# Row 5's last 640 columns are loaded by two transfers of their own

## The chip, the cores and the metric

The kernel runs on one core of one Trainium2 chip. The metric is the device time of one execution in microseconds, as the median of several runs. Before the change it is 1247.63 us, with three runs between 1247.31 and 1247.77 us.

## The reference

`logits` is 8 x 1024 x 8192 in float32 and `labels` is 8 x 1024 in int32 (they reach the kernel as 64-bit numbers). The result is the gradient of the cross entropy with respect to the logits, one softmax per row of 8192, with one subtracted at the label.

```python
logits_max = np.max(logits, axis=-1, keepdims=True)
exp_logits = np.exp(logits - logits_max)
softmax = exp_logits / np.sum(exp_logits, axis=-1, keepdims=True)
...
one_hot[batch_idx, seq_idx, labels] = 1.0

return (softmax - one_hot).astype(np.float32)
```

There are 8192 rows of 32 KB. Each is read once and written once, 268 MB each way.

## The kernel before, in words

The 8192 rows are taken 128 at a time, one row in each of the 128 partitions. What follows calls such a block of 128 x 8192 numbers (4 MB) a tile row, and counts them with t from 0 to 63. The wording of the change, "row 5", means the tile row t = 5. Two neighbouring tile rows, of parity j = 0 and 1, hold neighbouring rows of the logits.

The on-chip buffer `X` has six places (`SLOTS` = 3 times `G` = 2, so `R` = 6) of 32 KB in each partition. Tile row t uses place k = t % 6. Everything happens in place: a load fills it, VectorE finds the maximum of each row (`row_max`), ScalarE writes the exponentials over the logits and sums them (`row_exp`), VectorE inverts the sum (`invert`), ScalarE multiplies by the inverse (`row_scale`), VectorE subtracts one where the column number is the label (`subtract`), and a store sends it to the output.

All instructions are put out by one helper, `run` (in the profile nearly all of them are listed under line 67, where the helper calls the engine). It takes a list of waits; the last of them is carried by the instruction itself and each one ahead of it is an instruction of its own on the same engine. Then it lets the instruction count a semaphore up, by 16 for a transfer and by 1 for all else.

Each engine runs its own list in order:

- SP (SyncE) issues the 64 loads, in the order of t (`load`). From t = 6 on, each waits until the store from its place has landed (`put`). Tile rows 0 to 4 wait for nothing. Tile row 5 waits for VectorE, since the column numbers were first made in the first half of its place (`made`), from which VectorE copies them to PSUM (`iota`).
- VectorE makes the table of labels and the column numbers, then `row_max(0)`, and then passes a loop of ten rounds of six tile rows: `invert(k)`, `row_max` of the next tile row, `subtract(k)`. `row_max(5)` comes once in each round, at k = 4. Its load is awaited through the semaphore `got[2][1]`, against a count kept in a register.
- ScalarE runs `row_scale(k)` and `row_exp` of the next tile row, and issues the stores on its own queue.
- The last four tile rows, 60 to 63, stand behind the loop. The very last is scaled and subtracted in quarters and stored in two halves of 2 MB.

The names that the change touches are `load`, `row_max`, the line that makes the semaphores, and two constants at the head of the file (`LAST` is used nowhere).

Of the kernel before, what the change touches and what calls it, by code (L numbers as in the profile page):

```python
# [7 lines left out]
P = 128  # L8
G = 2
SLOTS = 3  # L10
R = SLOTS * G


LAST = 4


@with_exitstack
def kernel(
# [6 lines left out]
    nc = tc.nc  # L25
# [8 lines left out]
    N, V = x_nv.shape  # L34
# [3 lines left out]
    x_b = x_nv.rearrange("(b p j) v -> b p j v", p=P, j=G)  # L38
# [17 lines left out]
    with tc.tile_critical():  # L56
        sem = tc.alloc_semaphore
        got = [[sem(f"got{i}{q}") for q in range(2)] for i in range(SLOTS)]
        put = [[sem(f"put{i}{q}") for q in range(2)] for i in range(SLOTS)]
        lab_got, dve, pe, pool = (sem(n) for n in ("lab_got", "dve", "pe", "pool"))  # L60
        count = {}

        def run(engine, waits, counter, method, **operands):

            for w in waits[:-1]:
                engine.wait_ge(*w)
            instruction = getattr(engine, method)(**operands)  # L67
            for w in waits[-1:]:
                instruction._wait_ge(*w)
            step = 16 if method == "dma_start" else 1  # L70
            instruction.then_inc(counter, step)
            count[counter.name] = count.get(counter.name, 0) + step
            return counter, count[counter.name]
# [6 lines left out]
            out=ident[:], in_=ident[:], compare_op=Alu.not_equal, fill=1.0,  # L80
# [10 lines left out]
        for j in range(G):  # L91
            w = run(
                nc.tensor, [w_ident, w_lab], pe, "transpose",
                out=lab_ps[:, j, :], in_=lab_f[:, j, :], identity=ident[:],
# [4 lines left out]
            out=iota[:].bitcast(i32), in0=made.bitcast(i32), scalar1=0, scalar2=None, op0=Alu.bitwise_or,  # L99
# [6 lines left out]
        max_of, exp_of, inv_of, scl_of, sub_of = map(per_parity, ("max", "exp", "inv", "scl", "sub"))  # L106

        def slot(k):
            return X[:, k // G, k % G, :]

        def column(a, k):
            return a[:, k : k + 1]

        def load(t):
            b, j = divmod(t, G)
            k = t % R
            after = [(put[k // G][q], t // R * 16) for q in range(G)] if t >= R else []
            after = after[j : j + 1] or [w_iota] * (t == R - 1)
            run(nc.sync, after, got[k // G][j], "dma_start", out=slot(k), in_=x_b[b, :, j, :])

        def row_max(k, n):
            run(
                nc.vector, [(got[k // G][k % G], n)], max_of[k % G], "tensor_reduce",
                out=column(m, k), in_=slot(k), axis=mybir.AxisListType.X, op=Alu.max, negate=True,
            )

# [37 lines left out]
        for t in range(T):  # L164
            load(t)

        row_max(0, 16)
        row_exp(0, 1)

        done = [counter(nc.vector, q + 1) for q in range(SLOTS)]  # L170
        landed = counter(nc.vector, 16)
        with nc.vector.Fori(0, ROUNDS * SLOTS, SLOTS) as b:  # L172
            for k in range(R):
                invert(k, done[k // G])
                if k == R - 1:
                    nc.vector.reg_add(landed, landed, 16)
                row_max((k + 1) % R, landed)
                subtract(k, done[k // G], lab[:, k % G, bass.ds(b + k // G, 1)])
            for reg in done:
                nc.vector.reg_add(reg, reg, SLOTS)  # L180
# [13 lines left out]
        for t in range(ROUNDS * R, T - 1):  # L194
            k, n = t % R, t // G + 1
            invert(k, n)
            row_max(k + 1, 16 * (ROUNDS + 1))
            row_scale(k, n)
            row_exp(k + 1, n + k % G)
            subtract(k, n, lab[:, t % G, t // G : t // G + 1])  # L200
            store(k, n, o_b[t // G, :, t % G, :])
        k, n = (T - 1) % R, B
        invert(k, n)
        for q in range(4):
            c = slice(q * V // 4, (q + 1) * V // 4)
# [41 lines left out]
```

## Time and profile before

| What | Before |
|---|---|
| median of three runs | 1247.63 us |
| lowest and highest | 1247.31 and 1247.77 us |
| span of the profiled execution, first to last instruction | 1245.6 us |
| ACT: busy time | 919.4 us, 74% of the span |
| loads on SP's queue | 64 of 4096 KB |
| stores on ACT's queue | 63 of 4096 KB and 2 of 2048 KB |

The profile is of one execution, whose own time outside the profiler is not listed; its span stands 2.0 us below the median of the runs, which also count what lies around the span. The page gives busy times by engine, the span in 40 equal slices of 31.1 us, the DMA queues with their packets, and groups of instructions. A "landing" is the moment at which the last piece of a transfer has been counted on its semaphore. In the tables by stretch, a DMA packet is counted in the stretch in which it starts, so a share of the DMA engines can exceed 1.00 in a short stretch.

### The profile page before, as it was taken

To read this page: it belongs to the slowest core of one execution; us is meant where nothing else is said; L and a number is where in the kernel's file an instruction comes from. 1 tells how busy PE (TensorE), PEld (TensorE's weight loads), DVE (VectorE), ACT (ScalarE), POOL (GpSimd) and SP (SyncE) were. 2 spreads that over 40 slices of the span, in tenths; PEclk is the share of its full clock that TensorE was granted. 3 is DMA by queue.
4 is the path that set the end of the run, shared out by engine and by line. 5 is a ranking of instruction groups with operands and counts; after the bars stand their busy time and mean duration, and the time that the engine had idled before them with its cause. 6 is when DMAs were issued, how large, how long until landed. Compare 5 with 4: busy or idle time off the path is not lost.

```text
span 1245.6 us, 868 instructions
## 1 busy us (share of the span) xinstructions
PE 0.4 (0%) x2; PEld 0.3 (0%) x2; DVE 1121.8 (90%) x198; ACT 919.4 (74%) x196; POOL 7.4 (1%) x7
## 2 busy tenths in 40 slices
PE   0000000000000000000000000000000000000000
PEld 0000000000000000000000000000000000000000
DVE  5999999999988989889898898988988989889893
ACT  3888888888767777777767777677777777777772
POOL 2000000000000000000000000000000000000000
DMA  9999999999999999999999999999999999999999
GB/s 406 418 426 436 438 434 425 438 438 429 429 438 436 427 434 438 435 426 436 438 432 426 438 438 428 430 438 435 428 434 438 434 427 436 437 434 426 438 436 389
DMA packets 18625, 536.95 MB, mean 431 GB/s; under 512 B 2080, under 2 KB 2080, under 8 KB 2112
## 3 DMA queue, kind: packets, MB, share of 16 engines
q1 hardware_dynamic: 9216, 268.44, 50.0%
q10 hardware_dynamic: 9408, 268.51, 49.9%
q14 instruction: 1, 0.01, 0.0%
HBM read 268.50 MB, written 268.44 MB: 431 GB/s over the span
## 4 chain that ended last, share of the span: by engine, by line
another core or an unknown queue 67%; DVE 21%; DMA 6%; issue 2%; SPq 1%; DVEq 0%; ACT 0%; ACTq 0%; PE 0%
DVE m L67 11%; DVE X L67 10%; DMA out_dram<-X 4%; DMA X<-in_logits_dram 2%; SPq L67 1%; DVE iota L67 0%; DVE lab_f L67 0%; DMA lab_raw<-in_labels_dram 0%; DVEq L56 0%; ACT X L67 0%; DVE r L67 0%; PE iota L67 0%; ACTq L67 0%; DVEq L172 0%
## 5 line engine op out<-in xcount | busy, mean ns | idle before, releaser
L67 DVE TENSOR_REDUCE m<-X 128x1 f32<-128x8192 f32 x64 | 555.6, 8681 | 90.6 <-DMA X<-in_logits_dram 90.6
L67 ACT ACTIVATE X<-X,m 128x8192 f32<-128x8192 f32 x64 | 455.8, 7122 | 184.8 <-DVE m L67 184.8
L67 DVE SCALAR_TENSOR_TENSOR X<-iota,lab,X 128x8192 f32<-128x8192 int16 (+1 forms) x67 | 559.8, 8360 | 2.4 <-ACT X L67 2.4
L67 ACT ACTIVATE X<-X,r 128x8192 f32<-128x8192 f32 (+1 forms) x67 | 456.4, 6816 | 118.2 <-DVE r L67 118.2
L67 DVE RECIPROCAL r<-s 128x1 f32<-128x1 f32 x64 | 9.8, 153 | 7.3 <-ACT X L67 7.3
L67 ACT ACTIVATION_READ_ACCUMULATOR X<-X,m 128x1 f32 x64 | 11.9, 186 | 0.0
L67 DVE CAST lab_f<-lab_raw 32x256 f32<-32x256 int32 x1 | 3.8, 3784 | 4.6 <-DMA lab_raw<-in_labels_dram 4.6
L67 POOL IOTA X<- 128x8192 int16 x1 | 6.9, 6943 | 0.0
L67 DVE TENSOR_SCALAR iota<-X 128x4096 int32<-128x4096 int32 x1 | 4.4, 4428 | 0.1
L67 ACT ACT_TABLE_LOAD x1 | 1.3, 1283 | 1.4 <-SPq L56 1.4
L67 DVE COPY lab<-iota 128x64 f32<-128x64 f32 x1 | 0.2, 225 | 0.5 <-PE iota L67 0.5
L67 PE MATMUL iota<-ident,lab_f 32*128 32x32 f32 x2 | 0.4, 298 | 8.5 <-DVE lab_f L67 8.5
L67 PEld LDWEIGHTS iota<-ident,lab_f 32*128 32x128 f32 x2 | 0.3, 192 | 8.4 <-DVE lab_f L67 8.4
L67 POOL TENSOR_SCALAR_AFFINE_SELECT ident<-ident 32x32 f32<-32x32 f32 x1 | 0.2, 202 | 0.1
L67 POOL MEMSET ident<- 32x32 f32 x1 | 0.1, 114 | 0.5 <-SPq L56 0.5
L231 POOL MEMSET const-bfloat16-1.0<- 128x1 bf16 x1 | 0.1, 107 | 0.0
L231 POOL MEMSET const-uint8-127<- 128x1 uint8 x1 | 0.1, 107 | 0.0
L231 POOL MEMSET const-float32-0.0<- 128x1 f32 x1 | 0.1, 104 | 0.2 <-issue 0.2
L231 POOL MEMSET const-float32-1.0<- 128x1 f32 x1 | 0.1, 104 | 0.0
## 6 DMA issues: line engine op xcount, KB each, us to landing
X<-in_logits_dram SPq DMA_DIRECT2D x64, 4096.0 KB, 24.2
out_dram<-X ACTq DMA_DIRECT2D x63, 4096.0 KB, 55.2
out_dram<-X ACTq DMA_DIRECT2D x2, 2048.0 KB, 16.9
lab_raw<-in_labels_dram ACTq DMA_DIRECT2D x1, 64.0 KB, 3.7
```

What stands on the lines that cost most here:

```text
L67: instruction = getattr(engine, method)(**operands)
L231: nc = _bacc.Bacc("TRN2", target_bir_lowering=False, num_devices=1)
```

## The change: what it does

Tile row 5's first load (t = 5) brings columns 0 to 7551 of all 128 partitions. Two more transfers on SP's queue, directly behind it, bring columns 7552 to 8191: one for partitions 0 to 119 (120 pieces of 2560 bytes, 307,200 bytes) and one for partitions 120 to 127 (8 pieces of 2560 bytes, 20,480 bytes). Both count a new semaphore, `rest_got`, to 32 in all. `row_max(5)` waits for that 32 ahead of its old wait, in every round of the loop, though the semaphore is filled only once. All other loads of the kernel, those of the same place in later rounds among them, are as before.

```diff
-LAST = 4
+SLAB = 640
+MOST = 120
...
-        lab_got, dve, pe, pool = (sem(n) for n in ("lab_got", "dve", "pe", "pool"))
+        lab_got, dve, pe, pool, rest_got = (sem(n) for n in ("lab_got", "dve", "pe", "pool", "rest_got"))
...
-            run(nc.sync, after, got[k // G][j], "dma_start", out=slot(k), in_=x_b[b, :, j, :])
+            c = slice(0, V - SLAB) if t == R - 1 else slice(0, V)
+            run(nc.sync, after, got[k // G][j], "dma_start", out=slot(k)[:, c], in_=x_b[b, :, j, c])
+            if t == R - 1:
+                c = slice(V - SLAB, V)
+                for p in (slice(0, MOST), slice(MOST, P)):
+                    run(nc.sync, [], rest_got, "dma_start", out=slot(k)[p, c], in_=x_b[b, p, j, c])

         def row_max(k, n):
-            run(
-                nc.vector, [(got[k // G][k % G], n)], max_of[k % G], "tensor_reduce",
+            rest = [(rest_got, 32)] if k == R - 1 else []
+            run(
+                nc.vector, rest + [(got[k // G][k % G], n)], max_of[k % G], "tensor_reduce",
                 out=column(m, k), in_=slot(k), axis=mybir.AxisListType.X, op=Alu.max, negate=True,
             )
```

## The prediction

> **What bounds the kernel now.** The page comes first: its busy times, slices and queues.
>
> ```profile
> span 1245.6 us, 868 instructions
> PE 0.4 (0%) x2; PEld 0.3 (0%) x2; DVE 1121.8 (90%) x198; ACT 919.4 (74%) x196; POOL 7.4 (1%) x7
> ...
> GB/s 406 418 426 436 438 434 425 438 438 429 429 438 436 427 434 438 435 426 436 438 432 426 438 438 428 430 438 435 428 434 438 434 427 436 437 434 426 438 436 389
> DMA packets 18625, 536.95 MB, mean 431 GB/s; under 512 B 2080, under 2 KB 2080, under 8 KB 2112
> ...
> q1 hardware_dynamic: 9216, 268.44, 50.0%
> q10 hardware_dynamic: 9408, 268.51, 49.9%
> ...
> L67 DVE TENSOR_REDUCE m<-X 128x1 f32<-128x8192 f32 x64 | 555.6, 8681 | 90.6 <-DMA X<-in_logits_dram 90.6
> ```
>
> VectorE is busy 90%, but the 16 DMA engines carry loads (q1) and stores (q10) for 50.0% + 49.9% of their span. Every slice but the first and the last runs at 418 to 438 GB/s. By rounds of six tile rows (6 x 8.39 MB = 50.3 MB) the rate does not move at all; the third and the ninth round:
>
> ```profile
> 332.35:448.53 116.18, 0.00 (x0) 0.00 (x0) 104.50 (x19) 86.02 (x18) 0.00 (x0) 1.00 1.00 433
> ...
> 1029.40:1145.58 116.18, 0.00 (x0) 0.00 (x0) 104.39 (x19) 85.95 (x19) 0.00 (x0) 1.00 1.00 433
> ```
>
> The columns are length, busy us of PE, PEld, DVE, ACT and POOL, the granted clock, the DMA share and GB/s: 1.00 and 433 in both. That is 433 / 16 = 27.06 GB/s for one DMA engine, my price of a byte below.
>
> Next come the waits (us in total, times, longest) of SP and of VectorE, the first maximum that waited for a load, and the landings in the steady part of the run (loads first, then stores):
>
> ```profile
> SPq L67 <- DMA out_dram<-X: 1140.4, 58, 57.2
> ...
> DVE m L67 <- DMA X<-in_logits_dram: 90.6, 47, 2.0
> ...
> 307.22 8.69 DVE L67 TENSOR_REDUCE m<-X 128x1 f32<-128x8192 f32 x1 [0.54 <-DMA X<-in_logits_dram]
> ...
> DMA to landing us min/median/max: 24.2/24.2/24.3
> ...
> DMA to landing us min/median/max: 55.1/55.2/55.3
> ```
>
> SP always has a load ready and waits for a store to land. A load lands 24.2 us after its issue and a store 55.2 us, while a tile row takes 116.18 / 12 = 9.7 us of the DMA engines one way. So more than one load and several stores stand in the queues at any time. Compute could be tens of microseconds later without emptying them. The end is therefore set by bytes: the sixteen engines run without pause from the first load on, and the slowest of them ends the kernel.
>
> How far the slowest lies behind is seen in the last stores, in stretches of 0.05 us:
>
> ```profile
> 1242.85:1242.90 0.05, 0.00 (x0) 0.00 (x0) 0.00 (x0) 0.00 (x0) 0.00 (x0) 1.00 0.76 328
> 1242.90:1242.95 0.05, 0.00 (x0) 0.00 (x0) 0.00 (x0) 0.00 (x0) 0.00 (x0) 1.00 1.53 655
> 1242.95:1243.00 0.05, 0.00 (x0) 0.00 (x0) 0.00 (x0) 0.00 (x0) 0.00 (x0) 1.00 0.00 0
> 1243.00:1243.05 0.05, 0.00 (x0) 0.00 (x0) 0.00 (x0) 0.00 (x0) 0.00 (x0) 1.00 0.79 328
> 1243.05:1243.10 0.05, 0.00 (x0) 0.00 (x0) 0.00 (x0) 0.00 (x0) 0.00 (x0) 1.00 0.00 0
> 1243.10:1243.15 0.05, 0.00 (x0) 0.00 (x0) 0.00 (x0) 0.00 (x0) 0.00 (x0) 1.00 0.02 0
> 1243.15:1243.20 0.05, 0.00 (x0) 0.00 (x0) 0.00 (x0) 0.00 (x0) 0.00 (x0) 1.00 0.00 0
> 1243.20:1243.25 0.05, 0.00 (x0) 0.00 (x0) 0.00 (x0) 0.00 (x0) 0.00 (x0) 1.00 0.02 0
> 1243.25:1243.30 0.05, 0.00 (x0) 0.00 (x0) 0.00 (x0) 0.00 (x0) 0.00 (x0) 1.00 0.78 328
> 1243.30:1243.35 0.05, 0.00 (x0) 0.00 (x0) 0.00 (x0) 0.00 (x0) 0.00 (x0) 1.00 0.03 0
> ```
>
> A half row stored has packets of 16,384 bytes, and 328 GB/s for 0.05 us is one such packet. One packet starts in the first row, two in the second, one at 1243.00, then none for 0.2 us, and a single last one after 1243.25. So one engine is alone at the end, 0.20 to 0.30 us behind the next.
>
> **The change part by part.** The bytes of tile row 5 stay the same; only their split over engines and packets moves. Three things are to be costed.
>
> *Waits and issues.* The load of tile row 5, its landing, and its use (two rows of VectorE and SP in order of time, one of the transfer issued at 13.70):
>
> ```profile
> 13.70 0.33 SPq L67 DMA_DIRECT2D X<-in_logits_dram  x1
> ...
> 98.86 8.67 DVE L67 TENSOR_REDUCE m<-X 128x1 f32<-128x8192 f32 x1
> ...
> DMA to landing us min/median/max: 59.9/59.9/59.9
> ```
>
> It lands at 13.70 + 59.9 = 73.6 us and its maximum starts at 98.86, so 25 us are spare. Two more issues cost SP 2 x 0.33 = 0.66 us, right behind the first. Behind them on SP stands only the load of tile row 6, which waits for the first store; the earliest of the 58 waiting loads is issued at 71.2 us:
>
> ```profile
> L67 SPq DMA_DIRECT2D X<-in_logits_dram x58: 327/328/328, 71.2 to 1174.1; - x58
> ```
>
> So 56 us cover them. The wait for `rest_got` is a separate instruction on VectorE ahead of `row_max(5)`, ten times. Nothing in the trace before is that very wait. Below it costs nothing; above it costs what VectorE's queue shows near the loop's turn:
>
> ```profile
> 114.88 0.08 issue
> 114.95 0.06 DVEq L67
> ```
>
> That is 0.14 us, 1.4 us in ten rounds. Behind it stand `row_max(5)`, one `subtract`, and the store that ScalarE issues. I take 0: VectorE has 90.6 / 47 = 1.9 us idle in each tile row from 307 us on, and before that the queues' depth covers it. Without both covers it would be 1.4 us.
>
> *Bytes per engine.* The q1 row has 9216 packets for 64 loads, 144 each: 128 partitions and 16 completions, so a load falls on 16 engines with eight partitions each. The slab is 128 x 2560 = 327,680 bytes, 20,480 for each engine as it stands. If the 120 partitions go in eights to 15 engines, one engine is relieved of 20,480 / 27.06 = 0.757 us, and the last eight partitions go one each to eight engines, 2560 / 27.06 = 0.095 us more for these. The trace before has no transfer of 120 or 8 partitions, so the split itself is open; the rivals bound it. The Trainium skill (DMA: Bandwidth & Descriptors, "Why a DMA increments its semaphore by 16 and not by 1") says that the number of engines is the largest up to 16 that divides the outer dimension, taken from the lowest-numbered: that would be 15 and 8, which no transfer of this trace can test.
>
> *Packets.* Each engine gets some eight or nine data packets and two completions more. Their overhead is bounded by the last stores, of which three are whole and two are halves:
>
> ```profile
> 1196.33 0.35 ACTq L67 DMA_DIRECT2D out_dram<-X  x1
> ...
> 1215.68 0.34 ACTq L67 DMA_DIRECT2D out_dram<-X  x1
> ...
> 1222.74 4.86 ACTq L67 DMA_DIRECT2D out_dram<-X  x2
> ...
> DMA to landing us min/median/max: 19.0/28.6/38.3
> ...
> DMA to landing us min/median/max: 16.8/16.8/16.8
> ...
> DMA to landing us min/median/max: 17.1/17.1/17.1
> ```
>
> The whole ones land at 1196.33 + 28.6 = 1224.9 and 1215.68 + 19.0 = 1234.7, 9.75 apart; the halves at 1239.5 and 1222.74 + 4.86 - 0.34 + 17.1 = 1244.4, 9.7 later for both. Twice the packets cost 0 within the rounding of 0.1 us. Eleven packets: 0 to 0.14 us; I take 0.05.
>
> *The sum.* If the relieved engine is the one that ends last, the next one ends the kernel: -0.25 (middle of 0.20 to 0.30), plus 0.05 for packets, plus half of 0.095, as half of the engines carry one more piece: -0.15 us. If the late engine is another, the cost alone is left: 0.05 to 0.15, say +0.1 us. The rows do not name the late engine, so I hold both nearly even and lean to the first, as a single engine lies apart from the rest. The profiled span of 1245.6 becomes 1245.45; with the same 2.0 us around it the median of 1247.63 becomes 1247.5.
>
> By two rules of the Trainium skill this should cost time (DMA: Bandwidth & Descriptors, "Rules for kernel authors"): transfers to disjoint partitions are not worth splitting, and under 64 KB one pays mostly overhead; its fit in "Anatomy of one DMA" of about 2.0 us a transfer (for another issue path) would make 1247.6 + 4 = 1251.6. By that rule the trace disagrees: 130 transfers at 2 us each would be 260 us, and the rate of 433 GB/s leaves no such hole. That fixed part is latency, covered here.
>
> **The rivals.**
>
> 1. *The late engine is not the relieved one* (0.40): +0.1 us, 1247.7. For it: any of sixteen could be late.
>
> 2. *The slab collapses onto few engines, slower* (0.05). If 120 partitions fell on one engine, it would carry 307,200 - 20,480 = 286,720 bytes more, 10.6 us, and end last: 1258.2. On eight engines, 15 pieces each and one of the second transfer, it is 20,480 more and +0.76 us, 1248.4. It decides by more than 2.5 us below four engines (327,680 / 3 - 20,480 = 88,747 bytes, 3.3 us). For it: 120 is no multiple of 16. Against: nothing in the rows, only that 120 goes evenly into 15.
>
> 3. *Two short transfers show their latency, slower* (0.02). The nearest row is a transfer of 64 KB with nothing beside it:
>
> ```profile
> lab_raw<-in_labels_dram ACTq DMA_DIRECT2D x1, 64.0 KB, 3.7
> ```
>
> Twice 3.7 is 7.4 us, 1255.0. Against: the 25 us of cover, and tile row 6's load does not wait for them.
>
> 4. *The late engine costs in every tile row, faster* (0.03). If each load's wait for the sixteenth engine let the others idle, an engine on time would save up to 58 x 0.27 = 15.7 us: 1231.9. Against: DMA share 1.00.
>
> 5. *Nothing is moved* (0.04): the split ends with equal bytes per engine, 1247.6.
>
> **How the numbers follow.** The forecast, 1247.5 us, has 0.46. About 0.2% (2.5 us) is what a measurement of this kernel can tell from no change. Forecast, rival 1 and rival 5 stay inside it, as does rival 2 on eight engines (0.02 of its 0.05). That gives 0.92 for the same; 0.03 for faster (rival 4); 0.05 for slower (0.03 of rival 2, and rival 3). For the range, the runs shown scatter over 0.46 us; twice that, 0.9, below 1247.63 - 0.3 is 1246.4, and above 1247.63 + 0.35 (0.14 + 0.095 and some of the wait) is 1248.9. The +0.76 of rival 2 lies inside; the far ends 1231.9, 1255.0 and 1258.2 hold 0.08 together and stay out.
>
> **What would show it.** In the profile after, q1 keeps 268.44 MB and has 9216 + 128 packets and the completions of two transfers (1 to 16 each), 9346 to 9376 in all. By the skill's 15 and 8 engines it would be 9367. Rounds of 116.2 us at 433 GB/s, landings of 24.2 and 55.2 us, and row 5's maximum near 98.9 us should be as before. At the end, the lone last packet should have joined the others; if it is still 0.2 us behind, rival 1 is right. A landing of tile row 5's slab far behind its main part, or an end with several packets of one engine in a row, would show rival 2. A rate other than 433, or idle DMA behind 14 us, would make the whole argument wrong.

## The result, and the profile after

Over 21 runs of each the changed kernel takes 1249.21 us (1248.01 to 1255.93), the kernel before 1247.61 us (1247.24 to 1248.43). The ratio is 1.0017 with a 95% interval of 1.0010 to 1.0023: slower, by 1.6 us between the medians. That is less than the 2.5 us which the prediction took as the limit of a measurement, but the interval does not contain 1, and the median lies 0.3 us above the prediction's range. The runs spread much more than before: four lie between 1248.0 and 1248.4, fourteen between 1249.0 and 1249.7, three between 1253.6 and 1256. Of all runs in this document one, the 1272.29 us of after_later, counts as slow (over 1.5% above the fastest of its kernel) and enters no ratio.

The first profile is of one of the three (its own run took 1254.14 us); a second, of the unaltered changed kernel, is of the common kind (1249.36 us). From the page of the first, in the order of the rows shown of before:

```profile
span 1251.9 us, 880 instructions
...
GB/s 403 417 435 429 429 436 434 434 436 431 432 429 433 436 433 436 434 429 431 431 436 432 434 436 427 433 429 432 432 434 426 428 434 429 426 431 433 427 432 350
DMA packets 18776, 536.95 MB, mean 429 GB/s; under 512 B 2103, under 2 KB 2103, under 8 KB 2263
...
q1 hardware_dynamic: 9367, 268.44, 50.0%
...
L68 DVE TENSOR_REDUCE m<-X 128x1 f32<-128x8192 f32 x64 | 555.6, 8681 | 101.4 <-DMA X<-in_logits_dram 101.4
```

VectorE's wait for loads is 101.4 us in all, and was 90.6. The loads' queue has 9367 packets, 9216 + 128 + 15 + 8. So the long transfer ran on 15 engines and the short one on 8. That is what the Trainium skill gives (DMA: Bandwidth & Descriptors, "Why a DMA increments its semaphore by 16 and not by 1"), and the trace agrees further: `rest_got` has 25 separate counts, 15 + 8 from data and two, 67 us ahead of them, for the engines that take no part. Only this first profile has a lower rate in the late rounds. Its rows of the same stretches of one round, the sixth and the eighth:

```profile
680.88:797.05 116.17, 0.00 (x0) 0.00 (x0) 104.48 (x18) 85.22 (x19) 0.00 (x0) 1.00 1.00 432
...
913.23:1029.40 116.17, 0.00 (x0) 0.00 (x0) 103.01 (x19) 84.54 (x18) 0.00 (x0) 1.00 1.00 430
```

The engines stay busy, share 1.00, but move 430 GB/s and not 433: single packets take longer, up to 2.11 us in place of 1.21. What follows uses the second profile, of the common kind. Its issues by size with the time to landing, then its landings in the steady part (loads, then stores):

```profile
span 1247.2 us, 880 instructions
...
X<-in_logits_dram SPq DMA_DIRECT2D x1, 3776.0 KB, 60.3
X<-in_logits_dram SPq DMA_DIRECT2D x1, 300.0 KB
...
X<-in_logits_dram SPq DMA_DIRECT2D x1, 20.0 KB
```

```profile
DMA to landing us min/median/max: 29.7/30.3/30.9
...
DMA to landing us min/median/max: 48.6/49.2/49.7
```

Loads land 30.3 us after issue and stores 49.2; before it was 24.2 and 55.2. The split of one load, that of tile row 5, moved the whole rest of the run: loads are 6 us further back in the queues. Where this comes from is seen in the DMA queues between 72.6 and 81.3 us, first of the kernel before, then of the second profile after:

```profile
DMA packets 130, 3.74 MB, mean 429 GB/s; under 512 B 16, under 2 KB 16, under 8 KB 16
...
q10 hardware_dynamic: 66, 2.16, 57.5%
q1 hardware_dynamic: 64, 1.57, 41.9%
```

```profile
DMA packets 199, 3.49 MB, mean 401 GB/s; under 512 B 5, under 2 KB 5, under 8 KB 100
...
q10 hardware_dynamic: 98, 3.15, 83.7%
q1 hardware_dynamic: 101, 0.34, 9.6%
```

The columns are packets, MB and share. Each engine takes a store packet and a load packet in turn. Before, all but 16 counts of 4 bytes are 32 KB, and the two queues share the time. After, 95 of the 101 load packets are the slab's pieces of 2560 bytes (three are counts, three are 32 KB), and each waits for a whole store packet: one for one in number, 9.6% against 83.7% in time. By itself a piece is cheap: each of the 128 took 0.102 us, where 2560 bytes at 27.06 GB/s are 0.095. The Trainium skill says that engines go round their queues packet by packet (DMA: Bandwidth & Descriptors, "Queues, rings and completion order"); here a turn is one piece of a row.

The end of the last stores, in stretches of 0.2 us (82 GB/s is one packet of 16,384 bytes; stretches left out have none):

```profile
1243.40:1243.60 0.20, 0.00 (x0) 0.00 (x0) 0.00 (x0) 0.00 (x0) 0.00 (x0) 1.00 0.78 328
1243.60:1243.80 0.20, 0.00 (x0) 0.00 (x0) 0.00 (x0) 0.00 (x0) 0.00 (x0) 1.00 0.58 246
...
1244.00:1244.20 0.20, 0.00 (x0) 0.00 (x0) 0.00 (x0) 0.00 (x0) 0.00 (x0) 1.00 0.19 82
...
1244.60:1244.80 0.20, 0.00 (x0) 0.00 (x0) 0.00 (x0) 0.00 (x0) 0.00 (x0) 1.00 0.19 82
```

One engine is alone with its last two packets. Before, it was alone by 0.27 us with one. The last landing is at 1245.86 us (1244.35 before), 1.23 us behind the fifteenth (0.38 before). So 1.51 of the 1.7 us that this run loses are seen here: 0.85 in the one late engine, 0.66 in the others, whose fifteenth lands at 1244.63 (1243.96 before).

### The profile page after: what moved, and what is told of

It reads as the page before. It is cut to its first block, busy times and chain, and to the rows that moved or that the text cites. A ratio compares the mean times of both kernels' runs of the same rounds, so it can differ in the third digit from the quotient of the medians.

```text
span 1251.9 us, 880 instructions
## 1 busy us (share of the span) xinstructions
PE 0.4 (0%) x2; PEld 0.3 (0%) x2; DVE 1120.3 (89%) x198; ACT 919.3 (73%) x196; POOL 7.4 (1%) x7
## 3 DMA queue, kind: packets, MB, share of 16 engines
q1 hardware_dynamic: 9367, 268.44, 50.0%
## 4 chain that ended last, share of the span: by engine, by line
DMA 64%; DVE 26%; issue 8%; DVEq 0%; ACT 0%; ACTq 0%; PE 0%; SPq 0%
DMA out_dram<-X 38%; DMA X<-in_logits_dram 26%; DVE X L68 15%; DVE m L68 10%; DMA lab_raw<-in_labels_dram 0%; DVE iota L68 0%; DVEq L57 0%; ACT X L68 0%; DVE lab_f L68 0%; DVE r L68 0%; PE iota L68 0%; DVEq L179 0%; ACTq L68 0%; DVE lab L68 0%; DVEq L68 0%
## 5 line engine op out<-in xcount | busy, mean ns | idle before, releaser
L68 DVE TENSOR_REDUCE m<-X 128x1 f32<-128x8192 f32 x64 | 555.6, 8681 | 101.4 <-DMA X<-in_logits_dram 101.4
```

## The experiments

All runs were timed beside the kernel before on the same chip, whose medians were 1247.66 to 1247.69 us. The first four:

**after_again**: the changed kernel, unaltered.

> The changed kernel once more, unaltered, for a second profile of it. In its first profile loads land 31.8 us after issue and stores 48.2 us (before: 24.2 and 55.2), and DMA has a hole near the end of the stores. Theory A (the 2560-byte pieces of row 5 take turns with 32 KB store packets on each engine, one for one, so the loads fall some 7 us behind the stores for the rest of the run, and at the end too few stores are left to cover the last row's work): landings of 30 to 33 and 46 to 49 us again in the steady part, a hole of 1 to 2 us in the stores at the end, about 1249.2 us. Theory B (the engine that has no piece of the long transfer runs out of step, each landing waits for the last of 16, and that alone costs): the same time; this run cannot tell A from B.

1249.36 us, ratio 1.0019 (1.0009 to 1.0029). The landings came as expected. The hole in the stores did not: the last whole stores land 9.7 us apart without a break, and over half of the time is lost in the one late engine. So the second half of theory A does not hold for the common run. In the first profile there is such a hole as well (stretches of 0.5 us; the last number is GB/s):

```profile
1225.50:1226.00 0.50, 0.00 (x0) 0.00 (x0) 0.50 (x1) 0.00 (x0) 0.00 (x0) 1.00 0.61 262
1226.00:1226.50 0.50, 0.00 (x0) 0.00 (x0) 0.50 (x1) 0.00 (x0) 0.00 (x0) 1.00 0.00 0
1226.50:1227.00 0.50, 0.00 (x0) 0.00 (x0) 0.34 (x2) 0.00 (x0) 0.00 (x0) 1.00 0.30 131
```

**slab_whole**:

```diff
-                for p in (slice(0, MOST), slice(MOST, P)):
+                for p in (slice(0, P),):
...
-            rest = [(rest_got, 32)] if k == R - 1 else []
+            rest = [(rest_got, 16)] if k == R - 1 else []
```

> The 640 columns in one transfer of all 128 partitions, so all 16 engines get the same bytes and the same number of pieces. Theory A: the pieces still take turns with store packets, so landings near 31 and 48 us and a time near that of the changed kernel, 1248.3 to 1249.5. Theory B: no engine is out of step, so landings of 24.2 and 55.2 us and 1247.6 to 1247.8.

1249.22 us (1247.64 to 1254.24), ratio 1.0021 (1.0008 to 1.0034), with these landings:

```profile
DMA to landing us min/median/max: 32.8/33.4/34.0
...
DMA to landing us min/median/max: 45.6/46.1/46.7
```

Relieving one engine is not needed for the loss; with pieces on all 16 engines loads fall 9.2 us behind, and the median is the same. Theory B as stated falls. Two of the 10 runs, 1247.64 and 1247.74 us, are as fast as the kernel before; no profile shows what was different in them.

**slab_row0**:

```diff
-            c = slice(0, V - SLAB) if t == R - 1 else slice(0, V)
+            c = slice(0, V - SLAB) if t == 0 else slice(0, V)
...
-            if t == R - 1:
+            if t == 0:
...
-            rest = [(rest_got, 32)] if k == R - 1 else []
+            rest = [(rest_got, 32)] if isinstance(n, int) and n == 16 else []
```

> The same split of 640 columns into partitions 0 to 119 and 120 to 127, but of tile row 0, whose load runs with no store beside it; the extra wait stands only ahead of the very first maximum. Theory A: no store packets to take turns with, so landings stay at 24.2 and 55.2 us and the time at 1247.4 to 1247.9. Theory B: one engine is relieved by the same 20,480 bytes and is out of step from the start, so the time is near the changed kernel's, 1249, with longer landings.

1248.78 us (1248.01 to 1248.99), 1.1 us above the kernel before; the ratio, 1.0008 (0.9999 to 1.0016), leaves it open by itself, though only one of its 11 runs is below the highest of 33 before (1248.10). The landings are nearly the old ones:

```profile
DMA to landing us min/median/max: 24.2/24.5/25.4
...
DMA to landing us min/median/max: 54.1/55.0/55.3
```

There is next to no lag, and still a loss in ten of 11 runs. Theory A alone falls too.

**wait_alone**:

```diff
+            rest = [(lab_got, 16)] if k == R - 1 else []
             run(
-                nc.vector, [(got[k // G][k % G], n)], max_of[k % G], "tensor_reduce",
+                nc.vector, rest + [(got[k // G][k % G], n)], max_of[k % G], "tensor_reduce",
```

> The kernel before with only an extra wait ahead of row 5's maximum in each of the ten rounds (on the semaphore of the labels, long full); no load is split. Theories A and B: 1247.6, nothing. Theory C (the ten waits cost): up to 1.4 us, 1249.0, with the landings unchanged.

1247.97 us, ratio 1.0001 (0.9992 to 1.0010): no loss that can be told from none.

What the lossy ones share is in the trace's record of landings. Each transfer lands once for each engine. Here are the 16 landings of a store and a load near 670 us, in us from their median:

```
before       store  -0.23 -0.22 -0.18 -0.15 -0.10 -0.08 -0.04 -0.02 0.02 0.04 0.04 0.13 0.17 0.23 0.24 0.32
             load   -0.23 -0.22 -0.16 -0.15 -0.12 -0.06 -0.04 -0.01 0.01 0.04 0.06 0.16 0.17 0.23 0.24 0.33
after_again  store  -0.40 -0.32 -0.27 -0.24 -0.23 -0.12 -0.06 -0.01 0.01 0.59 0.97 1.70 1.71 1.72 1.78 4.77
             load   -4.66 -0.44 -0.42 -0.41 -0.36 -0.15 -0.09 -0.01 0.01 0.04 0.19 0.19 0.27 0.29 0.83 1.25
slab_row0    store  -1.36 -1.04 -0.11 -0.10 -0.09 -0.08 -0.06 -0.00 0.00 0.02 0.05 0.06 0.09 0.10 0.16 0.97
             load   -0.14 -0.13 -0.10 -0.09 -0.06 -0.04 -0.03 -0.00 0.00 0.04 0.05 0.06 0.15 0.95 1.04 1.33
```

Before, all engines land within 0.6 us, half a packet (1.21 us): they take load and store packets in one order. In after_again one engine is four packets ahead with loads and behind with stores: the relieved one, since one engine takes none of the 128 pieces, and in slab_whole, where none is relieved, none is ahead like this. Five stores, its own among them, land over a packet later than most. In slab_row0 two engines are one packet off. This made theory D, and theory S as its rival, for the next runs.

**slab_row0_whole**: as slab_row0, in one transfer of 128 partitions.

> The 640 columns of tile row 0 in one transfer of all 128 partitions: every engine gets the same bytes and pieces, and no store is in flight. Theory D (what costs is that some of the 16 DMA engines take load and store packets in another order than the rest, upon which the engine that ends last loses about twice as much per tile row): nothing disturbs the order here, so 1247.5 to 1247.9, landings of 24.2 and 55.2 us, and the last packet alone by 0.2 to 0.4 us. Theory S (a split load costs in itself, through its extra transfers or pieces): near slab_row0, 1248.5 to 1249.

1248.66 us (1248.26 to 1248.86), ratio 1.0007 (0.9998 to 1.0016). By the numbers this was theory S's outcome, and what I expected of D was wrong. The landings show why D itself need not fall: the order holds until the first store, and from the second store on two engines are a packet off, as in slab_row0.

**start_later_1, _2, _3**: no load is split; the first store only meets the loads at another moment. The number in the loop is 1, 2 or 3.

```diff
+        for _ in range(1):
+            w_turned = run(nc.vector, [w_turned], dve, "tensor_copy", out=lab[:], in_=lab_ps)
         w_iota = run(
```

> The kernel before with one more copy of the label table on VectorE (some 0.35 us) ahead of everything else there, so that the first store is issued that much later against the loads; no transfer is changed. A packet takes 1.21 us, so the first store meets the engines at another point of their packets. Theory D: if the engines' packet ends then lie on both sides of its arrival, some engines take one more load packet first, and the time rises to 1248.3 to 1249.5 with a last packet alone by over 1 us; if not, 1247.6. Theory S: 1247.6 in any case.

> As start_later_1 with two copies, some 0.7 us. Theory D: in one or two of the three shifts 1248.3 to 1249.5, else 1247.6. Theory S: 1247.6.

> As start_later_1 with three copies, some 1.05 us. Theory D: in one or two of the three shifts 1248.3 to 1249.5, else 1247.6. Theory S: 1247.6.

One copy took 0.26 us and not 0.35. One more: 1247.82 us, ratio 1.0002 (0.9993 to 1.0011). Two more: a median of 1247.68, ratio 1.0011 (0.9998 to 1.0024), but five of 11 runs from 1248.33 to 1255.92. Three more: 1248.69 us (1247.43 to 1251.41), ratio 1.0010 (1.0001 to 1.0019). So the loss, the scatter and even a run near 1256 appear with every transfer as before. Theory S falls as the sole cause: no split is needed. The profiles of one and of three copies, landings and end:

```profile
DMA to landing us min/median/max: 24.2/24.2/24.3
...
DMA to landing us min/median/max: 55.1/55.2/55.3
...
1242.80:1243.00 0.20, 0.00 (x0) 0.00 (x0) 0.00 (x0) 0.00 (x0) 0.00 (x0) 1.00 0.77 328
...
1243.20:1243.40 0.20, 0.00 (x0) 0.00 (x0) 0.00 (x0) 0.00 (x0) 0.00 (x0) 1.00 0.21 82
```

```profile
DMA to landing us min/median/max: 26.6/26.7/26.7
...
DMA to landing us min/median/max: 52.8/52.9/52.9
...
1243.40:1243.60 0.20, 0.00 (x0) 0.00 (x0) 0.00 (x0) 0.00 (x0) 0.00 (x0) 1.00 0.20 82
...
1244.00:1244.20 0.20, 0.00 (x0) 0.00 (x0) 0.00 (x0) 0.00 (x0) 0.00 (x0) 1.00 0.19 82
```

With three copies the loads settle two packets (2.4 us) later, the engines agree with one another, and still the late engine is alone for its last two packets. So the order among engines was not all. The last four runs set it (D1) against the offset of loads to stores (D2).

**start_later_5, start_later_9**: five and nine copies.

> The kernel before with five more copies of the label table (0.26 us each, 1.3 us in all, about one packet). Theory D1 (what costs is that the 16 engines differ from one another in the order of load and store packets): a shift by about one whole packet meets the engines at the same point again, so all keep one order: 1247.6 to 1247.9, last packet alone by 0.2 to 0.4 us. Theory D2 (what costs is any other offset between the load and the store stream than the one with landings of 24.2 and 55.2 us, also where all engines agree): the landings move by a packet or two and the time is 1248.3 to 1249.3 with a last packet alone by about 1 us; if the landings stay, 1247.6.

> As start_later_5 with nine copies (2.3 us, about two packets). Theory D1: 1247.6 to 1247.9 where all engines keep one order. Theory D2: 1247.6 only if landings stay at 24.2 and 55.2 us, else 1248.3 to 1249.3.

1250.05 us (1248.44 to 1265.40), ratio 1.0029 (1.0007 to 1.0051), and 1248.96 us, ratio 1.0009 (1.0000 to 1.0018). D1's return to 1247.6 did not come. In neither did the engines keep one order: stores of five copies land up to 2.7 us late on three engines, and of nine up to 1.2 us early. Neither tells D1 from D2; a whole packet more did not bring the old order back.

**row0_whole_later** (slab_row0_whole with two copies) and **after_later** (the changed kernel with two copies):

> slab_row0_whole (1248.66 us; two engines out of order from the second store on) with two copies of the label table, some 0.5 us, ahead on VectorE. Theories D1 and D2: the order is a matter of when stores and loads meet, so the same split load can come out at 1247.6 to 1247.9 with landings of 24.2 and 55.2 us in most runs, or be as scattered as start_later_2. Theory S (the split load costs in itself): 1248.5 to 1248.9, as without the copies.

> The changed kernel with two copies of the label table, some 0.5 us, ahead on VectorE. The 2560-byte pieces still take turns with store packets, so loads still fall 5 to 9 us behind (landings near 30 and 49 us) and engines differ by several packets. Theories D1 and D2: 1248.5 to 1250, no way back to 1247.6. A time of 1247.6 with these landings would refute both.

The first: 1248.32 us (1247.97 to 1252.49), ratio 1.0009 (1.0000 to 1.0018), scattered, with three runs at 1247.97 to 1248.01, so between the forecasts; its profile is of a run of 1249.58 us, in which one engine lands its loads 2.9 us behind the median. The second: a median of 1248.58 over 12 runs and of 1248.24 over the 11 that enter the ratio, with six between 1247.88 and 1248.24, and three at 1260.27, 1266.51 and 1272.29; ratio 1.0032 (1.0005 to 1.0060). Its profile is of one of the six, 1248.16 us:

```profile
DMA to landing us min/median/max: 28.6/29.1/29.5
...
DMA to landing us min/median/max: 49.9/50.4/50.8
...
1243.20:1243.40 0.20, 0.00 (x0) 0.00 (x0) 0.00 (x0) 0.00 (x0) 0.00 (x0) 1.00 0.39 164
...
1243.80:1244.00 0.20, 0.00 (x0) 0.00 (x0) 0.00 (x0) 0.00 (x0) 0.00 (x0) 1.00 0.19 82
```

Here the lag of 5 us is there and the relieved engine lands its loads 4.2 us ahead, but the other 15 engines agree within 0.85 us near 670 us; this run loses 0.5 us and not 1.7. So in this run the lag and the relief cost little by themselves. The median lies within the 1248.5 to 1250 that I had expected, but six runs do not.

The profiles side by side. "Stretch" is the time by which all load and store packets of 32 KB that start between 400 and 1100 us exceed the usual 1.213 us, added up over the 16 engines; "behind" is the last landing of the last store less the fifteenth:

| Profile | its run, us | loads / stores land after, us | stretch, us | behind, us |
|---|---|---|---|---|
| before | (span 1245.6) | 24.2 / 55.2 | 0.47 | 0.38 |
| start_later_2 | 1247.68 | 24.2 / 55.2 | 0.45 | 0.29 |
| start_later_1 | 1247.82 | 24.2 / 55.2 | 0.43 | 0.40 |
| wait_alone | 1248.01 | 24.2 / 55.2 | 0.48 | 0.45 |
| after_later | 1248.16 | 29.1 / 50.4 | 0.69 | 0.66 |
| start_later_3 | 1248.40 | 26.7 / 52.9 | 0.86 | 1.06 |
| slab_row0 | 1248.65 | 24.5 / 55.0 | 1.07 | 1.22 |
| slab_row0_whole | 1248.84 | 24.4 / 55.0 | 1.14 | 1.27 |
| start_later_9 | 1249.04 | 27.4 / 52.0 | 1.10 | 0.66 |
| slab_whole | 1249.30 | 33.4 / 46.1 | 0.99 | 1.22 |
| after_again | 1249.36 | 30.3 / 49.2 | 1.14 | 1.23 |
| row0_whole_later | 1249.58 | 29.0 / 50.4 | 1.17 | 0.97 |
| start_later_5 | 1250.05 | 26.7 / 52.8 | 1.15 | 1.33 |
| after, first profile | 1254.14 | 31.8 / 48.2 | 35.05 | 0.12 |

Wherever the pattern of before is undisturbed, the stretch is 0.43 to 0.48 us and the run takes at most 1248.01 us. In all others it is 0.69 or more, and the run longer. D1 and D2 each hold in part: start_later_3 loses with engines that agree but at another offset, slab_row0 at nearly the old offset with two engines out of order, and after_later, at another offset with 15 of 16 in order, loses least.

Nearly all of the stretch falls on one engine: in after_again the latest load landing goes from 1.21 us behind the median at 660 us to 2.04 at 1202, 1.07 us for each 700 us, against a stretch of 1.14. Before, the latest store goes from 0.38 at 689 us to 0.70 at 1193, 0.44 for each 700. Following the packets (each starts 3 or 4 ns before the one ahead of it on its engine ends) shows the same: in after_again, between 400 and 1100 us, one engine's packets lengthen and those of the other 15 keep 1.213 us. What is added is in its stores: 1.11 of the 1.14 us in after_again, 0.31 of the 0.47 before. In the first profile it is the reverse, 34.9 of 35.05 us in loads, and of all engines. One late engine is not all that is lost, either: in start_later_9, row0_whole_later and start_later_5 the fifteenth engine, too, lands only at 1245.32 to 1245.43 us, 1.4 us later than before.

Why the late engine's stores lengthen, and why the old pattern is the cheapest, stays open: no run shows it. Open too is why a few runs take 1253 us and more. Such runs occurred with and without a split, and never in the 122 runs of the kernel before, whose highest is 1248.43.

## Why the prediction was wrong, point by point

- **What bounds the kernel** was right: DMA engines without pause, the slowest of 16 ends it.
- **Waits and issues** were right: the ten waits alone cost nothing that can be told from zero, and the maximum of tile row 5 starts only 0.12 us later than before, as VectorE's row in order of time shows in the first profile:

```profile
98.98 8.66 DVE L68 TENSOR_REDUCE m<-X 128x1 f32<-128x8192 f32 x1
```

- **Bytes per engine** were right: 15 and 8 engines, 9367 packets.
- **The sum** is the step that failed. It took the late engine's lag, 0.20 to 0.30 us, as a constant from which to subtract, and gave all other engines 0.05 to 0.15 us of added work. The lag is the end of a drift of some 0.6 ns per us, and the drift more than doubled (0.44 to 1.07 us for each 700): landings show 0.38 us before and 1.23 after. With the fifteenth engine 0.66 us later, that makes the 1.5 us. Why the drift doubles stays open, as said above.
- **Packets** was priced by the wrong thing. Eleven packets at 0 to 0.14 us, taken from the last stores where no other transfer is in flight, is about right for the engine's own time: a row in two pieces takes 1.119 + 0.102 us in place of 1.213, 0.06 us for eight rows, and 0.10 for a ninth piece. What was left out is that beside stores each small load packet costs its queue a whole 32 KB turn. So loads fell 6 us behind and the 16 engines came to differ in their order. That this alone brought on the drift is not shown: start_later_3 has a stretch of 0.86 us without any small piece, and after_later only 0.69 with them.
- **The late engine** is not the relieved one after the change: the relieved engine lands its loads 4.66 us ahead of the median while the late one is 1.25 behind. Rival 1 had this right and its price, +0.1 us, wrong. Whether the engine that was late before is the one relieved, no trace shows.
- **Landings of 24.2 and 55.2 us** were named as what would show the steps right. They moved, which showed that something in the queues had changed; the rate of 433 GB/s, the other sign, held in the common run and would have hidden it.
- The rivals on the slower side (few engines, latency of short transfers) did not occur. The faster rival, 4, did not either. What did occur, a drift that grows when the order of packets is disturbed, was not on the list; the range missed the median by 0.3 us. That the loss stayed inside the 2.5 us to which the prediction gave 0.92 was luck: nothing in its working bounded the drift, and single runs lost 8 us.

## What to carry to other kernels

Where loads and stores share the DMA engines to the full, a transfer's price is not its bytes: here a piece of 2560 bytes took a turn against store packets of 32 KB, and its queue fell behind by 6 to 9 us. To split a load where no store is in flight kept the landings, but it was not free either: slab_row0 and slab_row0_whole lost 1.0 to 1.1 us between the medians. A kernel that is bound by DMA down to the last microsecond can rest on a regular order of packets over the engines. A change of when transfers meet, even 0.8 us on an engine that does not set the kernel's time, can break it, so compare many runs and look at the spread and at the times to landing, not at the rate alone.

## What the runs showed of the hardware that was not expected

The effect of one meeting lasts: tile row 5's pieces are through at 82 us, and the landings stay at 30.3 and 49.2 us for the rest of the run. With a delay of 0.5 us at the start and transfers identical to those before, runs of one kernel differ by 8.7 us (1247.27 to 1255.92, against 1247.24 to 1248.43 before); with the same delay runs of the changed kernel differ by 18.6 us (1247.88 to 1266.51). And one of the 16 engines drifts behind the others all through the run, by 0.44 us in 700 in the kernel before and by 1.07 in after_again, nearly all of it there in store packets.
